# Attention scores of the latent heads: three products of 96 rows become two of 128 rows and one of 32, the last for two PSUM banks from separate rows of the array

## The chip, the core and the metric

The kernel runs on one core of a Trainium2 chip. The metric is the device time of one execution in microseconds (us). TensorE (PE) multiplies; its weight loads stand in a row of their own in a profile (PEld) and run beside its products. VectorE (DVE), ScalarE (ACT) and GpSimd (POOL) do the rest, and SyncE (SP) issues most of the DMAs.

## The reference

A decoder block on 2048 tokens of width 1024: eight heads of attention with a forget gate ("fox"), eight heads of latent attention ("mla"), an output projection, and an MLP. All arithmetic is in float32. The change touches the scores of the mla heads alone:

```
mq = concat([q_nope, q_rope])      # 64 + 32 values per head and token
mk = concat([k_nope, k_rope])      # k_rope (32 values) is the same for all heads
logits = (mq . mk) * scale ; masked ; softmax ; p . v
```

## The kernel before, in words

A float32 product is made of rounded parts. Each operand is split into a high part and a low part ("hi", "lo"), and three products are added in PSUM: hi.hi, hi.lo and lo.hi. The fourth, lo.lo, is left out.

The part of the kernel that matters is the attention stage. It works in units, each of one head and 512 queries (`qb` from 0 to 3). Fox and mla units alternate, and mla runs two units behind. A unit has score steps and value steps. A score step (`step(j, c)`, lines 809 to 833) takes 128 queries and a chunk of up to 1024 keys:

- the products of `passes` (lines 210 to 213) into one bank of PSUM, if the chunk has up to 512 keys, and otherwise into two, with half of the chunk in each (line 820);
- on DVE the mask and the row's maximum (lines 825 and 828), on ACT the exponential (829), and on POOL the scaling of the probabilities (850).

The value steps turn the probabilities with transposes on PE (870), split them into hi and lo on ACT and DVE (lines 92 and 93), and multiply them by the values (887 and 888). At the end of a unit, ACT copies the result (892), a DMA on SP's queue moves its lower half to other partitions (893), POOL adds the halves (898), and SP stores them (899).

An mla head has four operand tiles: `a` (hi of q), `b` (hi of k), `c` (lo of q), `d` (lo of k), each with 64 rows of the plain part and 32 of the rotary part. So line 820 makes three products of 96 rows for each bank: a.b, a.d and c.b. A fox head has two products for each bank, of 128 and of 66 rows, because its tiles already pack hi and lo above each other.

Tiles come from two sets of slots. `s8` has 16 slots ("big", 8 KB for each partition) and gives the heads' tiles in turn, five for each head. `s4` has 21 slots ("mid", 4 KB) and gives the probabilities; three are held for other things, so that the other 18 go round. A tile can be loaded as soon as the last reader of the slot's earlier tile is done. `mid` and `big` (`ring`) take the next slot of the round.

The order of the score and value steps comes from a sorted list of due times (`add`), but a scheduler that lays out the program moves single instructions within it, DMAs above all. On each engine the order is fixed once the program is built. SP's queue is in order: a DMA that waits holds up those behind it.

Of the kernel before, what the change touches and what calls it, by code (L numbers as in the profile page):

```python
# [9 lines left out]
F32R = mybir.dt.float32r  # L10
# [8 lines left out]
P = 128  # L19
# [21 lines left out]
def f32v(ap):  # L41
    return ap.bitcast(F32)
# [3 lines left out]
def block_kernel(ctx, tc, x, positions, attn_norm_g, w_in, b_forget, q_norm_g, w_uq, kv_norm_g, w_ukv,  # L46
# [129 lines left out]
    def load_parts(kind, h, tiles, parts):  # L176

        a, b, c, d, v = tiles
        ld = nc.sync.dma_start
        s = slice(512 * parts[0], 512 * (parts[-1] + 1))  # L180
        tt = slice(4 * parts[0], 4 * (parts[-1] + 1))
        if kind == "fox":

            if a is not None:
                ld(f32v(a[0:HD, s]), fq[0][h, :, s])
                ld(f32v(a[HD:P, s]), fq[1][h, :, s])
                ld(f32v(b[0:HD, s]), fk[0][h, :, s])
                ld(f32v(b[HD:P, s]), fk[0][h, :, s])
                ld(f32v(c[0:HD, s]), fq[0][h, :, s])
                ld(f32v(d[0:HD, s]), fk[1][h, :, s])  # L190
        else:
            g, j = divmod(h, 4)
            for q, k, i2 in ((a, b, 0), (c, d, 1)):
                ld(f32v(q[0:HD, s]), mq[i2][h, :, s])
                ld(f32v(q[HD:QKD, s]), mr[i2][g, j * ROPE:(j + 1) * ROPE, s])
                ld(f32v(k[0:HD, s]), mk[i2][h, :, s])
                ld(f32v(k[HD:QKD, s]).rearrange("r (t k) -> r t k", k=P),
                   krd[i2].rearrange("g (t r) k -> r (g t) k", r=ROPE)[:, tt])
        if v is not None:
            load_v(kind, h, v, tt)  # L200

    def load_v(kind, h, v, tt):
        nc.sync.dma_start(f32v(v[:, tt]), (fv if kind == "fox" else mv).rearrange("(t p) h d -> h p t d", p=P)[h, :, tt])
# [6 lines left out]
    def passes(kind, a, b, c, d):  # L210
        if kind == "fox":
            return [(a, b, P), (c, d, HD + 2)]
        return [(a, b, QKD), (a, d, QKD), (c, b, QKD)]

# [31 lines left out]
    def mid(shape, dt=F32):  # L248
        return s4.ring(shape, dt)
# [509 lines left out]
    with ExitStack() as es:  # L759
# [2 lines left out]
        place = [room[0][:, i] for i in range(4)] + [t[:, i] for t in room[1:3] for i in range(2)]  # L762
        halves = [room[3][0:HD, i] for i in range(2)]
        turns, due, outs = [0], [], [0]
        pss = es.enter_context(tc.tile_pool(name="pss", bufs=2, space=PSUM))
        pspt = es.enter_context(tc.tile_pool(name="pspt", bufs=4, space=PSUM))

        def load_head(kind, h):
            if (kind, h) == ("fox", 0):
                tiles = first  # L770
                s8.put(*first)
            else:
                tiles = [big([P, S]) for _ in range(4)]
            v = big([P, NT, 2 * HD])
            if h:
                load_parts(kind, h, [*tiles, v], range(4))
                if kind == "fox":
                    load_decay(h, *tiles[2:])
            elif kind == "mla":
                for i in range(4):  # L780
                    load_parts(kind, h, [*tiles, v], [i])
            else:
                for i in range(4):
                    load_v(kind, h, v, slice(4 * i, 4 * i + 4))
            return passes(kind, *tiles), v

        def cuts(t):

# [6 lines left out]

        def score_steps(head, qb, st):

            ops, _ = head
            nch = qb // 2 + 1
            st["p"] = [[] for _ in range(QB)]  # L800
            negm = sma.tile([P, QB, nch], F32, name=f"negm{nch}")
            lsum = sma.tile([P, QB, nch], F32, name=f"lsum{nch}")
            fac = sma.tile([P, QB, nch], F32, name=f"fac{nch}")
            steps = []

            def step(j, c):
                t = QB * qb + j
                k0, k1 = cuts(t)[c]
                w = k1 - k0
                prob = mid([P, 1024])  # L810
                st["p"][j].append((k0, prob))
                nb = 1 if w <= 512 else 2
                wb = w // nb
                ps = pss.tile([P, 2, 512], F32, name="ps_s")
                qs = slice(t * P, (t + 1) * P)
                wm = max(wb, 256)
                for i in range(nb):
                    kb = k0 + i * wb
                    for n, (l, r, rows) in enumerate(ops):
                        nc.tensor.matmul(ps[:, i, 0:wm], l[0:rows, qs], r[0:rows, kb:kb + wm], start=(n == 0),  # L820
                                         stop=(n == len(ops) - 1))
                src = ps[:, 0:nb, 0:wb]
                if c == nch - 1:

                    nc.vector.tensor_tensor_reduce(src, src, maskb[:, 1024 - w:].rearrange("p (b w) -> p b w", b=nb),  # L825
                                                   -1.0, -NEG, ALU.add, ALU.min, negm[:, j, c:c + 1])
                else:
                    nc.vector.tensor_reduce(negm[:, j, c:c + 1], src, AX.XY, ALU.max, negate=True)
                nc.scalar.activation(prob[:, 0:w].rearrange("p (b w) -> p b w", b=nb), src, AF.Exp,  # L829
                                     scale=-1.0 if c == nch - 1 else 1.0,  # L830
                                     bias=negm[:, j, c:c + 1], accum_out=lsum[:, j, c:c + 1])
                if c == nch - 1:
                    norm(j)

            def norm(j):
                rl = sma.tile([P, 1], F32, name="rl")
                if nch == 1:
                    nc.vector.reciprocal(rl, lsum[:, j])
                else:
                    m = sma.tile([P, 1], F32, name="mmin")  # L840
                    nc.vector.tensor_reduce(m, negm[:, j], AX.X, ALU.min)
                    nc.scalar.activation(fac[:, j], negm[:, j], AF.Exp, scale=-1.0, bias=m)
                    l2 = sma.tile([P, nch], F32, name=f"l2{nch}")
                    l1 = sma.tile([P, 1], F32, name="l1")
                    nc.vector.tensor_tensor(l2, lsum[:, j], fac[:, j], ALU.mult)
                    nc.vector.tensor_reduce(l1, l2, AX.X, ALU.add)
                    nc.vector.reciprocal(rl, l1)  # L847
                for c, (k0, k1) in enumerate(cuts(QB * qb + j)):
                    pr = st["p"][j][c][1][:, 0:k1 - k0]
                    nc.gpsimd.tensor_scalar(pr, pr, rl, 1.0 if nch == 1 else fac[:, j, c:c + 1], ALU.mult, ALU.mult)  # L850

            for j in range(QB):
                for c in range(nch):
                    steps.append(lambda j=j, c=c: step(j, c))
            return steps

        def value_steps(head, row0, qb, st):
            _, v = head
            nk = QB * qb + QB
            steps = []  # L860

# [104 lines left out]
                f()  # L966
        for t, sl in zip(room, (s8, s4, s4, s4)):
            sl.put(t)


    pz = ctx.enter_context(tc.tile_pool(name="pz", bufs=1))
# [631 lines left out]
```

## Time and profile before

| what | value |
|---|---|
| time, median of 3 runs | 2951.94 us (2951.61 to 2952.47) |
| time of the profiled execution | 2952.62 us |
| its span, first to last instruction | 2950.8 us |
| first and last product of line 820 | 558.1 and 1424.3 us from the span's start |
| PE, DVE, ACT and POOL busy over the span | 95%, 77%, 47%, 46% |
| attention stage, 700 to 1300 us: PE, DVE, ACT, POOL busy | 595.92, 539.85, 492.57, 316.33 of 600 us |

The span and the time differ by 1.8 us, which lie outside the first and the last instruction. A busy PE is counted with modelled ends of its products, which overlap one another; how much of it is really used is read from the starts of neighbouring products.

### The profile page before, as it was taken

Reading aid. Unit: us, or ns where it says so; the run is one execution under the profiler, and the core shown is the slowest. Engines: PE = TensorE matmul, PEld = TensorE weight load, DVE = VectorE, ACT = ScalarE, POOL = GpSimd, SP = SyncE. Lnnn points to the kernel's source line nnn. Section 1 sums busy time; section 2 is a strip of 40 time slices with the busy share of each in tenths; the row PEclk is TensorE's granted clock in tenths of the full one; section 3 lists DMA queues with packets and bytes.
Section 4 is the critical chain, followed back from the end, with each engine's and each line's share of the span. In section 5 each row is a group of like instructions: output and inputs, shape, how many; then the busy total and the mean of one; then the engine's idle time right before and its main releaser. Section 6 shows DMA issues by size and latency. Waiting matters only on the chain. (4 is left out here: it accounts for less than half of the span.)

```text
span 2950.8 us, 40368 instructions
## 1 busy us (share of the span) xinstructions
PE 2804.3 (95%) x14378; PEld 2378.4 (81%) x14378; DVE 2267.7 (77%) x3573; ACT 1396.8 (47%) x2485; POOL 1355.0 (46%) x896
## 2 busy tenths in 40 slices
PE   7799979989999999998899899999999999999998
PEld 7678968878888888887788678888888788878886
DVE  7867786579889889988666756667666677897898
ACT  4144223478888888886533322233223433344432
POOL 3623353345555555557532246546555333453421
PEclk9999989999999999999999999999999999999998
DMA  5364435844435335332246454465444744465551
GB/s 141 129 217 163 152 108 187 242 104 111 91 92 121 78 92 120 92 94 60 76 154 214 171 186 157 150 235 214 157 151 165 283 148 150 149 217 178 206 193 57
DMA packets 262521, 442.94 MB, mean 150 GB/s; under 512 B 41712, under 2 KB 150384, under 8 KB 255600
## 3 DMA queue, kind: packets, MB, share of 16 engines
q1 hardware_dynamic: 206848, 300.75, 34.8%
q10 hardware_dynamic: 55472, 139.61, 12.4%
q8 instruction: 114, 1.87, 0.3%
q14 instruction: 87, 0.71, 0.1%
HBM read 275.54 MB, written 156.37 MB: 146 GB/s over the span
## 5 line engine op out<-in xcount | busy, mean ns | idle before, releaser
L1260 PE MATMUL mm<-big,mid 128*128 128x512 f32 x2688 | 619.5, 392 | 17.2 <-ACT big L1335 6.9
L1260 PEld LDWEIGHTS mm<-big,mid 128*128 128x128 f32 x2688 | 506.0, 189 | 129.6 <-ACT big L1335 12.0
L127 PE MATMUL mm<-big,mid 128*128 128x512 f32 x1312 | 515.8, 394 | 8.1 <-DVE mid L236 6.5
L126 PE MATMUL mm<-big,big 128*128 128x512 f32 (+2 forms) x1160 | 437.6, 377 | 0.9 <-DVE big L236 0.9
L820 PE MATMUL ps_s<-big,big 96*128 96x384 f32 (+11 forms) x1720 | 415.4, 368 | 8.0 <-ACT mid L829 7.8
L125 PE MATMUL mm<-big,big 128*128 128x512 f32 (+2 forms) x1072 | 405.7, 378 | 12.3 <-DVE krf L388 9.8
L850 POOL TENSOR_SCALAR mid<-mid,rl,fac 128x768 f32<-128x768 f32 (+4 forms) x256 | 255.9, 1009 | 268.1 <-DVE rl L847 83.3
L829 ACT ACTIVATE mid<-ps_s,negm 128x896 f32<-128x896 f32 (+7 forms) x384 | 333.0, 868 | 93.0 <-DVE negm L825 43.6
L242 POOL TENSOR_TENSOR mid<-mid,mid 128x1024 f32<-128x1024 f32 x88 | 238.5, 2710 | 296.2 <-DVE mid L576 94.9
L235 ACT ACTIVATE big<-mid 128x1024 fp32r<-128x1024 f32 x218 | 214.9, 1049 | 319.5 <-PE mm L126 200.2
L870 PE MATMUL ps_t<-ident,mid 128*128 128x128 f32 x2176 | 339.3, 274 | 8.3 <-POOL mid L850 7.4
L870 PEld LDWEIGHTS ps_t<-ident,mid 128*128 128x128 f32 x2176 | 273.4, 141 | 63.7 <-POOL mid L850 8.2
L820 PEld LDWEIGHTS ps_s<-big,big 96*128 96x128 f32 (+2 forms) x1720 | 287.3, 192 | 30.9 <-ACT mid L829 11.8
L1171 POOL TENSOR_TENSOR mid<-mid,mid 128x1024 f32<-128x1024 f32 x60 | 199.3, 3347 | 230.8 <-DVE big L236 198.6
L127 PEld LDWEIGHTS mm<-big,mid 128*128 128x128 f32 x1312 | 249.2, 190 | 61.9 <-DVE mid L236 7.4
L236 DVE TENSOR_TENSOR mid<-mid,mid 128x1024 fp32r<-128x1024 f32 x112 | 204.5, 1850 | 116.0 <-ACT mid L235 80.1
L93 DVE TENSOR_TENSOR big<-ps_t,big 128x512 fp32r<-128x512 f32 (+3 forms) x427 | 253.7, 602 | 37.9 <-ACT big L92 34.8
L92 ACT ACTIVATE big<-ps_t 128x512 fp32r<-128x512 f32 (+3 forms) x427 | 224.8, 535 | 72.2 <-PE ps_t L870 64.9
L126 PEld LDWEIGHTS mm<-big,big 128*128 128x128 f32 x1160 | 221.8, 191 | 37.6 <-DVE big L236 1.8
L825 DVE CUSTOM_DVE_ANT_0 ps_s<-ps_s,maskb 128x768 f32<-128x768 f32 (+7 forms) x256 | 227.9, 891 | 21.5 <-PE ps_s L820 19.5
L125 PEld LDWEIGHTS mm<-big,big 128*128 128x128 f32 x1072 | 205.0, 191 | 46.3 <-DVE krf L388 10.8
L125 PE MATMUL mm<-big,mid 128*128 128x512 f32 x528 | 211.5, 401 | 6.9 <-ACT mid L991 2.4
(213 smaller groups left out, 5272.9 us busy)
## 6 DMA issues: line engine op xcount, KB each, us to landing
gd<-mid ACTq DMA_DIRECT2D x109, 512.0 KB, 3.0
mid<-gd SPq DMA_DIRECT2D x109, 512.0 KB, 3.8
mid<-in_w_up SPq DMA_DIRECT2D x64, 512.0 KB, 5.5
mid<-in_w_down SPq DMA_DIRECT2D x64, 512.0 KB, 5.1
mid<-in_x SPq DMA_DIRECT2D x32, 512.0 KB, 4.1
xd<-mid ACTq DMA_DIRECT2D x28, 512.0 KB, 2.8
big<-xd SPq DMA_DIRECT2D x14, 1024.0 KB, 8.8
mid<-in_w_in SPq DMA_DIRECT2D x24, 512.0 KB, 4.7
```

Of the source, the lines that this page charges most:

```text
L92: nc.scalar.activation(hi, ps, AF.Copy)
L93: nc.vector.tensor_tensor(lo, ps, f32v(hi), ALU.subtract)
L125: nc.tensor.matmul(ps, lh, rh, start=(k == 0), stop=False)
L126: nc.tensor.matmul(ps, lh, rl, start=False, stop=False)
L127: nc.tensor.matmul(ps, ll, rh, start=False, stop=(k == nk - 1))
L242: (eng or nc.gpsimd).tensor_tensor(t, raws[a], raws[b], op)
L820: nc.tensor.matmul(ps[:, i, 0:wm], l[0:rows, qs], r[0:rows, kb:kb + wm], start=(n == 0), stop=(n == len(ops) - 1))
L825: nc.vector.tensor_tensor_reduce(src, src, maskb[:, 1024 - w:].rearrange("p (b w) -> p b w", b=nb), -1.0, -NEG, ALU.add, ALU.min, negm[:, ...
L829: nc.scalar.activation(prob[:, 0:w].rearrange("p (b w) -> p b w", b=nb), src, AF.Exp, scale=-1.0 if c == nch - 1 else 1.0, bias=negm[:, j, ...
L850: nc.gpsimd.tensor_scalar(pr, pr, rl, 1.0 if nch == 1 else fac[:, j, c:c + 1], ALU.mult, ALU.mult)
L870: nc.tensor.transpose(ps[:, j * P:(j + 1) * P], prob[:, kt * P - k0:(kt + 1) * P - k0], ident)
L1260: nc.tensor.matmul(ps[:, m], l[:, k, tk(m)], r[:, :, tk(k)], start=(first and k == n == 0), stop=(k == 3 and n == 2), skip_group_check=True)
```

## The change

`passes` gives two products of 128 rows for an mla head. Tile `a` now holds q_nope hi above q_nope lo, and `b` holds k_nope hi twice, so that a.b is hi.hi + lo.hi of the plain part. Tile `c` holds q_nope hi, q_rope hi and q_rope lo (64 + 32 + 32 rows), and `d` holds k_nope lo and k_rope hi twice, so that c.d is hi.lo of the plain part, and hi.hi + lo.hi of the rotary part. What is left is hi.lo of the rotary part, a product of 32 rows. Its operands are `r_hi`, a new "mid" tile for each mla unit (q_rope hi, loaded twice, to rows 0 to 31 and 32 to 63), and `kr_lo`, a new "big" tile that is held during the whole stage (k_rope lo, also twice). For a chunk with two banks, the first bank uses rows 0 to 31 and the second rows 32 to 63, and the two instructions stand next to each other behind the products of 128 rows of both banks.

```diff
-            for q, k, i2 in ((a, b, 0), (c, d, 1)):
-                ld(f32v(q[0:HD, s]), mq[i2][h, :, s])
-                ld(f32v(q[HD:QKD, s]), mr[i2][g, j * ROPE:(j + 1) * ROPE, s])
-                ld(f32v(k[0:HD, s]), mk[i2][h, :, s])
-                ld(f32v(k[HD:QKD, s]).rearrange("r (t k) -> r t k", k=P),
-                   krd[i2].rearrange("g (t r) k -> r (g t) k", r=ROPE)[:, tt])
+            rows = [slice(HD + n * ROPE, HD + (n + 1) * ROPE) for n in range(2)]
+            for n in range(2):
+                ld(f32v(a[n * HD:(n + 1) * HD, s]), mq[n][h, :, s])
+                ld(f32v(b[n * HD:(n + 1) * HD, s]), mk[0][h, :, s])
+                ld(f32v(c[rows[n], s]), mr[n][g, j * ROPE:(j + 1) * ROPE, s])
+                load_rope(d[rows[n]], 0, parts)
+            ld(f32v(c[0:HD, s]), mq[0][h, :, s])
+            ld(f32v(d[0:HD, s]), mk[1][h, :, s])
...
+    def load_rope(dst, n, parts):
+        s, tt = slice(512 * parts[0], 512 * (parts[-1] + 1)), slice(4 * parts[0], 4 * (parts[-1] + 1))
+        nc.sync.dma_start(f32v(dst[:, s]).rearrange("r (t k) -> r t k", k=P),
+                          krd[n].rearrange("g (t r) k -> r (g t) k", r=ROPE)[:, tt])
...
-        return [(a, b, QKD), (a, d, QKD), (c, b, QKD)]
+        return [(a, b, P), (c, d, P)]
...
+        kr_lo = s8.get([P, S])
...
+                    for n in range(2):
+                        load_rope(kr_lo[n * ROPE:(n + 1) * ROPE], 1, [i])
...
+            r_hi = None
+            if mla is not None:
+                r_hi = mid([P, 512], F32R)
+                g, h4 = divmod(mla, 4)
+                for n in range(2):
+                    nc.sync.dma_start(f32v(r_hi[n * ROPE:(n + 1) * ROPE]),
+                                      mr[0][g, h4 * ROPE:(h4 + 1) * ROPE, 512 * qb:512 * (qb + 1)])
...
-                                         stop=(n == len(ops) - 1))
+                                         stop=(r_hi is None and n == len(ops) - 1))
+                for i in range(nb if r_hi is not None else 0):
+                    kb, rows = k0 + i * wb, slice(i * ROPE, (i + 1) * ROPE)
+                    nc.tensor.matmul(ps[:, i, 0:wm], r_hi[rows, tk(j)], kr_lo[rows, kb:kb + wm], start=False, stop=True)
```

The line numbers of the changed kernel are higher by 20 to 24: its score products stand in line 840, the new ones in 845, the transposes in 894, the value products in 911 and 912, the move of a unit's half in 917, its store in 923, and the loads of `r_hi` in 818.

How the instructions stand at three places follows. The first is on PE, where a step of an mla unit (head 2, second unit) is made; before:

```order
L820 MATMUL ps_s_8824<-big_4_8260,big_5_8259 128x320
L820 MATMUL ps_s_8824<-big_3_8262,big_5_8259 128x320
L820 MATMUL ps_s_8824<-big_4_8260,big_0_8261 128x320
L820 MATMUL ps_s_8824<-big_4_8260,big_5_8259 128x320
L820 MATMUL ps_s_8824<-big_3_8262,big_5_8259 128x320
L820 MATMUL ps_s_8824<-big_4_8260,big_0_8261 128x320
```

That is one step with two banks of 320 keys: three products for each. The same kind of step now, with what stands ahead of it (`big_7` is `kr_lo`, `mid_20_8637` is `r_hi`):

```order
L911 MATMUL ps_t_8498<-mid_0_5199,big_4_7373 128x384
L894 MATMUL ps_t_8663<-ident_63,mid_2_8265 128x128
L840 MATMUL ps_s_8644<-big_3_8303,big_0_8302 128x320
L840 MATMUL ps_s_8644<-big_8_8305,big_15_8304 128x320
L840 MATMUL ps_s_8644<-big_3_8303,big_0_8302 128x320
L840 MATMUL ps_s_8644<-big_8_8305,big_15_8304 128x320
L845 MATMUL ps_s_8644<-big_7_5202,mid_20_8637 128x320 x2
L912 MATMUL ps_t_8498<-mid_0_5199,big_4_7373 128x384
```

There are as many instructions as before, but the last two take their operands from 32 rows each, and they are neighbours. The second place is on PE directly ahead of those rows. `r_hi` takes slot 20 of the round, whose earlier tile, `mid_20_8159`, is a probability tile; the first row is its last reader:

```order
L894 MATMUL ps_t_8629<-ident_63,mid_20_8159 128x128
L894 MATMUL ps_t_8629<-ident_63,mid_9_8211 128x128
L894 MATMUL ps_t_8629<-ident_63,mid_2_8265 128x128
L840 MATMUL ps_s_8602<-big_1_7370,big_13_7369 128x512
L840 MATMUL ps_s_8602<-big_5_7372,big_2_7371 128x512
L840 MATMUL ps_s_8602<-big_1_7370,big_13_7369 128x512
L840 MATMUL ps_s_8602<-big_5_7372,big_2_7371 128x512
L912 MATMUL ps_t_8498<-big_12_5198,big_4_7373 128x512
L894 MATMUL ps_t_8656<-ident_63,mid_9_8211 128x128
L894 MATMUL ps_t_8656<-ident_63,mid_2_8265 128x128
L911 MATMUL ps_t_8498<-big_12_5198,big_4_7373 128x512
L912 MATMUL ps_t_8498<-big_12_5198,big_4_7373 128x512
```

So 17 instructions lie between the one that frees the slot and the pair that reads what is loaded into it. It is so for the second unit of heads 1 to 6; the other units have 27 or more between them. The third place is SP's queue at the start of the stage, where the first mla head's tiles (`big_1`, `big_2`, `big_5`, `big_6`, `big_13`) and then the second fox head's are loaded; before, the first unit's half (L893) stands behind the fox loads:

```order
L203 DMA big_2_5516<-mv_85 128x4x128
L185 DMA big_5_5941<-fq0_71 64x2048
L186 DMA big_5_5941<-fq1_72 64x2048
L187 DMA big_4_5942<-fk0_73 64x2048
L188 DMA big_4_5942<-fk0_73 64x2048
L189 DMA big_0_5943<-fq0_71 64x2048
L190 DMA big_3_5944<-fk1_74 64x2048
L207 DMA big_3_5944<-fb_76 2x16x128
L203 DMA big_7_5208<-fv_75 128x4x128
L893 DMA mid_13_5201<-mid_16_5200 64x512
```

Now it (L917) stands ahead of the last mla loads, and so ahead of the fox loads; the second unit's half stands behind them:

```order
L917 DMA mid_13_5201<-mid_16_5200 64x512
L197 DMA big_13_5514<-mk0_83 64x512
L198 DMA big_1_5515<-mr1_82 32x512
L208 DMA big_2_5516<-krd0_77 32x4x128
L212 DMA big_14_5209<-fv_75 128x4x128
L200 DMA big_1_5515<-mq0_79 64x512
L201 DMA big_2_5516<-mk1_84 64x512
L212 DMA big_5_5517<-mv_85 128x4x128
L185 DMA big_4_5964<-fq0_71 64x2048
L186 DMA big_4_5964<-fq1_72 64x2048
L187 DMA big_0_5965<-fk0_73 64x2048
```

The move of the first unit's half has passed the fox loads and some of the mla loads. Over the whole program SP issues 817 DMAs instead of 723.

## Rows read from the trace of the kernel before

**Rows 1.** The page: busy time, share of the span and instructions of each engine.
```profile
PE 2804.3 (95%) x14378; PEld 2378.4 (81%) x14378; DVE 2267.7 (77%) x3573; ACT 1396.8 (47%) x2485; POOL 1355.0 (46%) x896
```

**Rows 2.** Stretches of the attention stage, from:to, length, busy us of each engine.
```profile
core 0: us, PE busy (x) PEld busy (x) DVE busy (x) ACT busy (x) POOL busy (x), PEclk, DMA share, GB/s
555.00:600.00 45.00, 34.27 (x217) 29.84 (x215) 30.27 (x82) 24.59 (x62) 11.95 (x14) 0.90 0.93 251
700.00:1300.00 600.00, 595.92 (x3670) 521.68 (x3670) 539.85 (x1365) 492.57 (x1134) 316.33 (x327) 1.00 0.43 100
1300.00:1400.00 100.00, 89.03 (x519) 76.93 (x518) 87.91 (x188) 70.66 (x160) 70.49 (x62) 0.95 0.22 63
```

**Rows 3.** What PE waited for, 700 to 1300 us: total us, times, longest.
```profile
PE ps_s L820 <- ACT mid L829: 1.9, 5, 0.4
PE ps_t L888 <- DVE big L93: 1.0, 4, 0.3
PE ps_t L888 <- DVE mid L93: 0.5, 2, 0.2
```

**Rows 4.** Groups of 560 to 1425 us, shapes apart: the mla score products by width.
```profile
L820 PE MATMUL ps_s<-big,big 96*128 96x512 f32 x240 | 67.4, 411 | 0.3 <-ACT mid L829 0.3
L820 PE MATMUL ps_s<-big,big 96*128 96x448 f32 x240 | 58.3, 377 | 0.0
L820 PE MATMUL ps_s<-big,big 96*128 96x384 f32 x264 | 57.2, 349 | 0.1
L820 PE MATMUL ps_s<-big,big 96*128 96x320 f32 x240 | 45.7, 326 | 0.0
L820 PE MATMUL ps_s<-big,big 96*128 96x256 f32 x48 | 10.0, 318 | 0.5 <-ACT mid L829 0.5
```

**Rows 5.** PE in order of time: start, length, line; neighbouring starts give the pace.
```profile
902.12 0.39 PE L888 MATMUL ps_t<-mid,big 128*128 128x512 f32 x1
902.34 0.39 PE L887 MATMUL ps_t<-big,big 128*128 128x512 f32 x1
902.57 0.27 PE L870 MATMUL ps_t<-ident,mid 128*128 128x128 f32 x1
...
907.06 0.34 PE L888 MATMUL ps_t<-big,big 128*128 128x384 f32 x1
907.24 0.28 PE L887 MATMUL ps_t<-big,big 128*128 128x256 f32 x1
907.35 0.60 PE L870 MATMUL ps_t<-ident,mid 128*128 128x128 f32 x4
...
909.07 1.04 PE L870 MATMUL ps_t<-ident,mid 128*128 128x128 f32 x8
909.86 0.48 PE L888 MATMUL ps_t<-big,big 128*128 128x512 f32 x1
```

**Rows 6.** PE in order of time around a fox step, 128 and 66 rows in turn.
```profile
936.12 1.18 PE L820 MATMUL ps_s<-big,big 128*128 128x512 f32 x4
937.14 0.40 PE L888 MATMUL ps_t<-mid,big 128*128 128x512 f32 x1
```

**Rows 7.** Weight loads in order of time.
```profile
907.68 0.19 PEld L888 LDWEIGHTS ps_t<-big,big 128*128 128x128 f32 x1
907.79 0.19 PEld L887 LDWEIGHTS ps_t<-mid,big 128*128 128x128 f32 x1
907.91 0.19 PEld L888 LDWEIGHTS ps_t<-mid,big 128*128 128x128 f32 x1
```

**Rows 8.** Line 893, the small DMA of SP's queue: ns, and us from issue to landing.
```profile
L893 SPq DMA_DIRECT2D mid<-mid x64: 461/491/1472, 585.5 to 1475.8; - x64
DMA to landing us min/median/max: 2.2/2.3/12.6
```

**Rows 9.** The start of the stage: SP's DMA, POOL's wait for it, PE's wait behind.
```profile
585.53 0.53 SPq L893 DMA_DIRECT2D mid<-mid  x1
599.17 1.25 POOL L898 TENSOR_TENSOR mid<-mid,mid 64x512 f32<-64x512 f32 x1 [7.38 <-DMA mid<-mid]
601.34 0.47 PE L870 MATMUL ps_t<-ident,mid 128*128 128x128 f32 x1 [6.37 <-POOL mid L850]
```

More of the change, by code (lines that the diff above doesn't have):

```diff
@@ L784, in load_head @@
                     load_v(kind, h, v, slice(4 * i, 4 * i + 4))
-            return passes(kind, *tiles), v
+            return passes(kind, *tiles), v, None if kind == "fox" else h
         def cuts(t):
@@ L796, in score_steps @@
         def score_steps(head, qb, st):
-            ops, _ = head
+            ops, _, mla = head
             nch = qb // 2 + 1
+            r_hi = None
[5 more added lines that the diff above has]
+                                      mr[0][g, h4 * ROPE:(h4 + 1) * ROPE, 512 * qb:512 * (qb + 1)])
             st["p"] = [[] for _ in range(QB)]
@@ L857, in value_steps @@
         def value_steps(head, row0, qb, st):
-            _, v = head
+            _, v, _ = head
             nk = QB * qb + QB
@@ L968, in block_kernel @@
             sl.put(t)
+        s8.put(kr_lo)
     pz = ctx.enter_context(tc.tile_pool(name="pz", bufs=1))
```

## The prediction, made before the changed kernel ran

> **What bounds the kernel now.** Read the page first: PE is busy for 95% of the span, and the next engine, DVE, for 77% [rows 1]. That share is a mean over stages, so the second view is the table of stretches: between 700 and 1300 us, the even part of the attention stage, PE is busy for 595.92 of 600 us, DVE for 539.85, ACT for 492.57 [rows 2]. Third, the waits of that stretch: PE waited for 3.4 us in all [rows 3]. A busy PE is counted with modelled ends, so the fourth view is the order of time, where neighbouring starts give the pace: a product of 512 columns starts 0.22 to 0.23 us before the next, one of 384 columns 0.18 and one of 256 columns 0.11 [rows 5]. These are the columns at one pace and next to nothing besides. So PE is the bound here, and what leaves its queue shortens the stage. At both ends of the stage it is not so: PE is busy for 34.27 of 45 us at the start and 89.03 of 100 us near the end [rows 2].
>
> **What goes.** The number of score products stays. Of an mla step with two banks, six products of 128 or 96 rows become four and a pair of 32 rows; if the two of a pair run side by side, PE's queue is shorter by one product. The mla products are counted by width: 240 of 512 columns, 240 of 448, 264 of 384, 240 of 320, 48 of 256 [rows 4]; a third of each is the number of banks. Steps with one bank (five for each head, of widths 256, 256, 384, 512 and 512) keep three products. That leaves, for all heads, pairs of banks: 40 of 320 columns, 40 of 384, 40 of 448 and 32 of 512, which is 152 products saved. Prices by pace: 0.23 us for 512 and 0.18 for 384 [rows 5]; between those and the 0.11 of 256 I take 0.205 for 448 and 0.145 for 320. The sum is 32 x 0.23 + 40 x (0.205 + 0.18 + 0.145) = 28.6 us.
>
> Whether a pair does run side by side is shown by no row, since nothing in this trace uses 32 rows. From below a second product costs 0 (both start together), from above its whole 0.145 to 0.23 us. I take the lower end: the two share neither rows nor a bank, and weight loads already run beside products. The Trainium skill (TensorE: Matmul & The Clock Gate, Part 3) says that products in different strips of 32 rows run at once and start about 4 ns apart; by that the pairs would cost 152 x 0.004 = 0.6 us, an estimate from that page.
>
> **What is added on PE.** First, weight loads. They follow each other every 0.11 us [rows 7]. A pair needs two, 0.22 us, and only the product ahead covers them: 0.145 us at 320 columns, 0.18 at 384, 0.205 at 448, 0.23 at 512. If no load runs further ahead, 40 x (0.075 + 0.04 + 0.015) = 5.2 us stand open; if it does, 0. I take 3, near the middle, since a load can be fetched early but not always.
>
> Second, the change between 128 and 32 rows. There are 24 steps for each head, 192 in all, with two changes each, so 384. From below a change costs nothing: fox products of 128 and 66 rows alternate, and four of 512 columns take 1.02 us to the next start [rows 6], 0.255 each, of which the first carries what transposes leave open (a product behind eight transposes starts 0.79 us after the first of them [rows 5], less than eight times 0.11). From above it costs what neighbouring products now overlap, 0.39 us of length less 0.23 of pace, 0.16 us [rows 5]: 61 us in all. The nearest row is that of the fox step, also a change of rows, so I take 0; the upper end is a rival below.
>
> **What is added beside PE.** Each mla unit loads `r_hi` by two DMAs of SP's queue, 64 in all, behind which the loads of heads and the moves of unit results are queued. Their issue is about 0.49 us and landing 2.3 us after it [rows 8], so the second half is there some 2.8 us after the slot is free. For the second unit of heads 1 to 6 the slot is freed only 17 instructions ahead of the pair: two transposes, four products of 512, three more, two transposes, one product of 384, one transpose and four of 320, at the prices above 5 x 0.11 + 7 x 0.23 + 0.18 + 4 x 0.145 = 2.9 us. It is a tie: 0 to 0.5 us for each of six units, 0 to 3 us; I take 1. A unit that waits holds up PE's transposes and value products too, since PE's queue is in order. Other units have 27 or more instructions, 4 us and up, so 0.
>
> The heads' loads grow from 384 to 512 rows, and `kr_lo` takes one of the slots, so a fox head's last operand tile is loaded later than before, but still well over a hundred PE instructions ahead; DMA engines are busy for 0.43 in the even part [rows 2]. I take 0.
>
> At the start DMA is full (0.93 [rows 2]), and more is loaded there: 18 more issues on SP (eight of the first mla head, eight of `kr_lo`, two of `r_hi`), at about 0.5 us each, 9 us, delay the loads of the second fox head, which is read only after the first mla unit. But the move of the first unit's half no longer stands behind the fox loads. Before it was issued at 585.53, POOL's addition began only at 599.17, after 7.38 us of waiting, and PE stood for 6.37 us behind that [rows 9]. The second unit's half now stands behind the same loads instead, so the wait may move on as well as go. From -6 to +6 us; I take 0.
>
> **What eats into the gain.** DVE has 60 us free of 600 [rows 2]; with PE's part shorter by some 3%, its share rises from 90% to 93%, and short waits of PE get more frequent. For them I take a tenth of the gain, 3 us (0 to 10). Near the end (1300 to 1400 us) PE already has 11 us free, so half of the last head's share, 28.6 / 8 / 2 = 1.8 us, is lost.
>
> **The sum.** -28.6 + 3 + 0 + 1 + 0 + 3 + 1.8 = -19.8 us. The profiled execution took 2952.6 us, of which the span was 2950.8 and 1.8 lie outside it; that stands 0.7 us over the median of the runs, 2951.9. So 2932.8 by the profiled execution, 2932.1 by the median; I say 2933.
>
> **The rivals.** The first ends on the other side: each change between 128 and 32 rows empties the array, so that the next product cannot start until the last has left. For it speaks the length of a product over its pace, 0.16 us [rows 5], which must be hidden somehow; against it the free alternation of 128 and 66 rows [rows 6], which may however be one and the same setting. The place is the two ends of every pair. It decides from 19.8 / 384 = 0.05 us for each change; at 0.16 us the time is 2933 + 61 = 2994. If the weight loads too wait for the empty array, 0.11 us more for each change [rows 7], 42 us, it is 3036. The Trainium skill (TensorEngine Tiling (Array Packing), Tiling Modes) says that changing the tiling mode, as against the tile, drains TensorE; it gives no time for it. No row of this trace can show it agree or not.
>
> Second, the change doesn't do what it says: the two of a pair run one after the other. Then 28.6 us are not won, and only the small costs are left: 2952.6 + 1 = 2954, or up to 2957 with open weight loads. For it: no row with two products at once. Against it: separate rows and banks.
>
> Third, the changes cost a part, 0.03 to 0.06 us, and the gain is mostly gone: 2944 to 2956.
>
> Fourth, the gain is there on PE, but DVE and ACT, whose steps each chunk needs in turn, take over as the bound: of 28.6 us a third is left, and 2943 comes out. For it: DVE at 90% and ACT at 82% in the even part [rows 2]; against it: PE waited for 3.4 us of 600 [rows 3].
>
> **How the numbers follow.** My forecast has 0.40, with 2922 to 2945 as its own range: the lower end with no open weight loads, no lost tenth and the wait at the start gone, the upper end with the small costs at their bounds. Draining at 0.06 us or more has 0.32, the pair in series 0.09, the partial cost 0.12 and DVE as the bound 0.07. Faster by over 0.2% (under 2946; about 0.2% is what a measurement of this kernel can tell from no change): the forecast, the fourth and a part of the third, 0.51. Within 0.2%: the rest of the third and most of the second, 0.15. Slower: 0.34. The range goes from 2922 to 2998, so that the drain at its price of 0.16 us lies in it, and the drain with open weight loads does not (0.12); 0.04 lie below.
>
> **What would show it.** In order of time, the two of a pair start within some 0.02 us, and the next product follows one pace after: step right. A start of the second a whole pace after the first: the second rival. A gap ahead of the pair and behind it that no wait explains: the first; PE's count of busy us in the stage would then not fall. Waits of PE's line 845 for a DMA, in the second units of heads: the tie went wrong. DVE or ACT as what PE waits for, well over 3.4 us in 600: the fourth. A stage between first and last score product (866 us now) that is not some 20 us shorter makes the prediction wrong.

## The result: 3.1% slower

The changed kernel takes 3044.23 us (median of 4 runs, 3042.51 to 3047.0), the kernel before 2951.78 (4 runs, 2950.85 to 2952.47). The ratio is 1.0314 with an interval of 1.0296 to 1.0332: 92 us more, where 19 less were forecast. The time lies outside the range.

Nearly all of it lies in the attention stage: line 840's first and last product stand at 559.6 and 1513.7 us, 954 us apart, where they were 866 apart. What comes behind is 1 us longer than before.

The page after, to be set beside [rows 1]:

```profile
PE 2864.3 (94%) x14378; PEld 2359.4 (78%) x14378; DVE 2264.8 (74%) x3573; ACT 1401.0 (46%) x2485; POOL 1355.3 (45%) x896
```

PE has as many instructions as before and 60 us more of busy time, although 304 of its products run in pairs. The stretches of the stage, with the columns of [rows 2]:

```profile
555.00:600.00 45.00, 37.06 (x230) 32.09 (x228) 31.70 (x81) 24.07 (x60) 14.65 (x17) 0.92 0.91 261
700.00:1300.00 600.00, 566.24 (x3248) 450.03 (x3246) 477.39 (x1206) 439.06 (x1004) 279.95 (x287) 0.97 0.45 102
1300.00:1400.00 100.00, 92.95 (x533) 73.94 (x533) 78.07 (x196) 71.57 (x164) 44.41 (x49) 0.97 0.39 88
```

In the even part PE starts 3248 products in 600 us instead of 3670, stands for 34 us instead of 4, and is granted 0.97 of its clock instead of 1.00. The start of the stage is a little better than before. Two things have to be told apart here: PE that is busy and gets less done, and PE that waits.

**Busy and slower.** The order of time around a pair, PE and its weight loads (PEld) after, in the place of [rows 5, 6]:

```profile
972.99 0.83 PE L840 MATMUL ps_s<-big,big 128*128 128x320 f32 x4
...
973.75 0.18 PEld L845 LDWEIGHTS ps_s<-big,mid 32*128 32x128 f32 x2 [0.19 <-issue]
973.75 0.41 PE L845 MATMUL ps_s<-big,mid 32*128 32x320 f32 x2
974.10 0.19 PEld L912 LDWEIGHTS ps_t<-big,big 128*128 128x128 f32 x1 [0.16 <-DVE rl L871]
974.10 0.44 PE L912 MATMUL ps_t<-big,big 128*128 128x384 f32 x1
...
974.38 0.49 PE L894 MATMUL ps_t<-ident,mid 128*128 128x128 f32 x3
```

The two of the pair share one start (the single records are 0.003 us apart). But from their start to the next product 0.35 us go by, for 320 columns that take 0.145 at the pace of the prediction. The value product behind them, of 384 columns, takes 0.28 to the next start instead of 0.18. And the weight loads of both start when the product itself does (973.75, 974.10), not during the product ahead. No wait on another engine's work explains it: the release named is "issue", or an instruction of DVE that had ended at 973.86, 0.24 us before.

**Waiting.** What PE waited for from 700 to 1300 us, in the place of [rows 3]:

```profile
PE ps_s L845 <- DMA mid<-mr: 27.6, 10, 5.0
PE ps_t L912 <- DVE big L93: 2.3, 6, 0.5
PE ps_t L912 <- DVE mid L93: 1.6, 4, 0.6
```

The new wait is the one for `r_hi`; the others are hardly changed. From 555 to 1530 us it comes to 34.4 us in 13 waits. Six of them are near 5 us, one for each of heads 1 to 6; the other seven, 0.6 to 1.3 us, belong to first units but for one. One of the six, in order of time on SP's queue and on PE:

```profile
741.85 0.31 SPq L818 DMA_DIRECT2D mid<-mr  x1
...
745.51 0.31 SPq L818 DMA_DIRECT2D mid<-mr  x1
...
749.16 0.70 PE L840 MATMUL ps_s<-big,big 128*128 128x512 f32 x2
...
754.38 0.79 PE L845 MATMUL ps_s<-big,mid 32*128 32x512 f32 x1 [4.51 <-DMA mid<-mr]
...
755.10 0.80 PE L912 MATMUL ps_t<-big,big 128*128 128x512 f32 x1
```

This is the third unit of its head, not the second. The first half of `r_hi` was issued at 741.85, behind the next mla head's loads, and PE goes on 12.5 us later. The last of those loads was issued at 737.41 and landed at 753.86, `r_hi` behind it at 754.34. From 732 to 755 us the packets of queue q1 take 90.1% of the time of the 16 DMA engines:

```profile
q1 hardware_dynamic: 2912, 4.72, 90.1%
```

The line's own record, beside [rows 8], says the same of the worst landing:

```profile
L818 SPq DMA_DIRECT2D mid<-mr x64: 307/323/852, 460.2 to 1480.6; - x64
...
DMA to landing us min/median/max: 1.8/3.4/12.5
```

What follows the wait is as dear again by half. A product of 512 columns now lasts 0.80 us instead of 0.39 [rows 5]. The stretches behind two of the six waits:

```profile
755.00:760.00 5.00, 5.00 (x18) 3.82 (x17) 2.04 (x4) 1.87 (x4) 2.45 (x3) 0.50 0.34 78
875.00:880.00 5.00, 5.00 (x18) 3.82 (x17) 2.04 (x4) 1.86 (x4) 2.56 (x3) 0.50 0.34 78
```

The granted clock is 0.50 there, the level of 1.2 GHz, after PE had stood for 4.5 to 5 us; the six such stretches have 0.50 to 0.59. Five us at half clock are 2.5 us of work, six times some 15 us, an estimate from these rows.

At the start of the stage the move of the first unit's half is issued at 582.62 instead of 585.53. POOL's addition, which waits for it, begins at 595.64 instead of 599.17 and without the 7.38 us of waiting, and no product behind it waits for POOL, where one stood for 6.37 us [rows 9]:

```profile
582.62 0.50 SPq L917 DMA_DIRECT2D mid<-mid  x1
...
595.64 1.26 POOL L922 TENSOR_TENSOR mid<-mid,mid 64x512 f32<-64x512 f32 x1
```

### The profile page after: what moved, and what is told of

Read it like the earlier page. It is cut to its first block, busy times and chain, and to the rows that moved or that the text cites. A ratio compares the mean times of both kernels' runs of the same rounds, so it can differ in the third digit from the quotient of the medians.

```text
span 3041.6 us, 40519 instructions
## 1 busy us (share of the span) xinstructions
PE 2864.3 (94%) x14378; PEld 2359.4 (78%) x14378; DVE 2264.8 (74%) x3573; ACT 1401.0 (46%) x2485; POOL 1355.3 (45%) x896
## 5 line engine op out<-in xcount | busy, mean ns | idle before, releaser
L840 PE MATMUL ps_s<-big,big 128*128 128x384 f32 (+4 forms) x1376 | 355.5, 376 | 3.2 <-ACT mid L853 3.0
L894 PE MATMUL ps_t<-ident,mid 128*128 128x128 f32 x2176 | 348.6, 278 | 3.0 <-POOL mid L874 2.7
L840 PEld LDWEIGHTS ps_s<-big,big 128*128 128x128 f32 x1376 | 228.3, 194 | 19.3 <-ACT mid L853 5.7
```

The source lines that it names most:

```text
L894: nc.tensor.transpose(ps[:, j * P:(j + 1) * P], prob[:, kt * P - k0:(kt + 1) * P - k0], ident)
```

## The experiments

Each kernel ran beside the kernel before on the same chip. "us more" or "less" of a kernel by itself is its ratio to before, times 2952; between two kernels, the difference of their ratios. Such a difference has an interval of 7 to 11 us either way.

Beside the time, the order of the steps matters. The traces give it as a list, between the first and the last score product, of transposes, value products by width and score steps by width. "In common" is the share of two such lists that stands in the same order in both.

### Without the late r_hi: the pair, full rows, the same rows, nothing (e1 to e4)

e1 loads `r_hi` two units ahead into tiles of its own, two mid slots that leave the round:

```diff
+        early = [s4.get([P, 2, 512]) for _ in range(2)]
+
+        def r_hi_of(k):
+            return early[k // 2 % 2][:, k % 2]
...
-                r_hi = mid([P, 512], F32R)
...
+                k = 4 * mla + qb
+                r_hi = r_hi_of(k)
+                for ahead in ((0, 1, 2) if k == 0 else (2,)):
+                    fetch_r_hi(k + ahead)
```

> The changed kernel, but r_hi has four tiles of its own and is loaded two units ahead. Theory: two costs ate the gain, the change between 128 and 32 rows (0.09 us for the array to empty and 0.11 for an uncovered weight load, 384 times, 76 us) and the late r_hi (PE waited 34.4 us for it, and ran at a granted clock of 0.50 behind the six long waits, some 3 us each). Without the second, 3044 - 34 - 18 = 2992 us (2985 to 3000), and no wait of PE for this DMA. Rival (the waits only take the place of others, all is in the row changes): 3030 us or more. Rival (late data is most of it): under 2965 us.

Measured: 2973.18 us, ratio 1.0066 (1.0044 to 1.0087). PE's waits for `r_hi` are gone. All three guesses missed: it is 73 us under the changed kernel, where the theory had 52, one rival 14 or less and the other over 79. But two slots leave the round here, which changes the order too (e5 to e12). e2 is e1 with a third product of 128 rows for each bank (`kr_lo` zero below its 32 rows), so that nothing changes rows and nothing runs in pairs:

```diff
-                    kb, rows = k0 + i * wb, slice(i * ROPE, (i + 1) * ROPE)
+                    kb, rows = k0 + i * wb, slice(0, P)
```

> As the run before, with r_hi early, but the third product has 128 rows for either bank, of which rows 32 to 127 are zero: the same products, tiles and order, no change between row counts, no pair. Theory (the row change costs 0.2 us each time): as the kernel before, 2950 to 2960 us, and next to no gaps around the third product. Rival (the gaps come with the product's place, its operands or its bank, not with its rows): 2952 + 76 = 3028 us or so.

Measured: 2920.69 us, ratio 0.9888 (0.9862 to 0.9915). So the pair with its changes of rows costs 52 us more than the full rows that it was to improve on, with nearly the same order on PE (99% in common). But e2 is also 33 us faster than before, which neither theory had, and which e5 takes up. e3 is e1 with both small products in rows 0 to 31, so that they can't run side by side:

```diff
-                    kb, rows = k0 + i * wb, slice(i * ROPE, (i + 1) * ROPE)
+                    kb, rows = k0 + i * wb, slice(0, ROPE)
```

> r_hi early, and both products of 32 rows use rows 0 to 31, so that they cannot run side by side; the number of changes between 128 and 32 rows is the same. Theory (the pair does run side by side and saves 28 us): 28 us over the run with r_hi early, or more if the second weight load is uncovered too (152 x 0.1 = 15 us). Rival (the pair saves nothing): the same time as the run with r_hi early.

Measured: 3002.23 us, ratio 1.0159 (1.0128 to 1.0191), 27 us over e1 by the ratios, with the very same order: as expected, the pair does save its 28 us. The price of the change of rows can be read between e2 and e3, whose order on PE is nearly the same (99% in common). PE in order of time, a step with two banks of 448 columns, and the weight load of the product behind it; e2:

```profile
970.76 1.06 PE L853 MATMUL ps_s<-big,big 128*128 128x448 f32 x4
971.66 0.57 PE L858 MATMUL ps_s<-big,mid 128*128 128x448 f32 x2
971.87 0.19 PEld L924 LDWEIGHTS ps_t<-big,big 128*128 128x128 f32 x1
972.07 0.39 PE L924 MATMUL ps_t<-big,big 128*128 128x512 f32 x1
```

and e3:

```profile
965.61 1.06 PE L850 MATMUL ps_s<-big,big 128*128 128x448 f32 x4
966.60 0.68 PE L855 MATMUL ps_s<-big,mid 32*128 32x448 f32 x2
967.20 0.19 PEld L922 LDWEIGHTS ps_t<-big,big 128*128 128x128 f32 x1 [0.32 <-issue]
967.21 0.38 PE L922 MATMUL ps_t<-big,big 128*128 128x256 f32 x1
```

The small products start 0.99 us behind the four large ones instead of 0.90, and the product after them 0.61 us later instead of 0.41. So 0.09 us go on entering the section of 32 rows, and 0.20 inside it and on leaving: 0.11 [rows 7] for the weight load that starts only with the product, which leaves 0.09. The 0.10 that the next product loses was seen above: its weight load, which in e2 begins 0.20 us ahead of it, begins with it here. That is 0.39 us for a step, 0.2 for each change, and for 192 steps 75 us; less the 28 of the pairs, 47 are left, and 52 were measured. The single records of all the sections of e1 and e3 give the same at every width, a median of 0.09 us on entering, 0.19 inside and on leaving, and 0.10 at the product behind (0.06 where that has 128 columns).

e4 leaves the third product out, and with it q_rope hi by k_rope lo; it shows what leaving that product out gives:

```diff
-            if mla is not None:
+            if False:
                 r_hi = mid([P, 512], F32R)
```

> Leaves out the product of hi of the rotary query and lo of the rotary key (the third product of each bank), and with it r_hi; two products of 128 rows for each bank are left. Theory (PE's queue bounds the stage, a product saved is time saved): 344 products of mean 0.185 us, 63 us less than before, 2888 us (2885 to 2900). Rival (DVE takes over as the bound): half of it, 2920 us.

Measured: 2909.74 us, ratio 0.9851 (0.983 to 0.9872). Of the 63 us only 44 come out. The order on PE has 92% in common with the kernel before, so this is no clean price of the products. And PE waits again from 700 to 1300 us:

```profile
PE ps_t L912 <- DVE l L870: 13.0, 6, 2.8
PE ps_t L912 <- DVE big L93: 2.1, 4, 0.5
```

### The order of the steps (e5, e10, e11, e12)

e5 is the kernel before, with its three products of 96 rows, and three slots held out of the rounds, unused:

```diff
+        held = [s8.get([P, S]), *[s4.get([P, 2, 512]) for _ in range(2)]]
```

> The kernel before, with its three products of 96 rows, but with three slots taken out of the rounds for the whole stage (one big, two mid) and nothing put into them, as many as the kernel with 128-row third products (2920.7 us, ratio 0.989) holds. With fewer slots the same score and value steps come in another order on PE, much the order of that kernel. Theory A (that kernel's gain of 33 us over before is the order of the steps, not the packing): 2915 to 2930 us, ratio 0.988 to 0.993. Rival B (128 rows in place of 96, or the other loads, give it): the time of before, ratio 0.997 to 1.003.

Measured: 2928.54 us, ratio 0.9907 (0.9887 to 0.9927). Theory A: 27 of e2's 33 us come with no change of arithmetic at all, and the order on PE has 97% in common with e2, where the kernel before has 86%. The even part of e5, with the columns of [rows 2]:

```profile
700.00:1300.00 600.00, 599.83 (x3753) 533.39 (x3752) 540.58 (x1391) 502.25 (x1159) 319.96 (x330) 1.00 0.43 100
```

PE starts 3753 products in 600 us instead of 3670, 2.3% more. The 4 us in which PE stood idle are gone; the other 9 or 10 us come of products that start sooner behind one another, which I did not split further. e10 holds only the two mid slots, e11 four mid slots, and e12 is e2 with two more:

```diff
+        held8, held4 = [s8.get([P, S]) for _ in range(0)], [s4.get([P, 2, 512]) for _ in range(2)]
```

> The kernel before with two mid slots held out and unused, and no big one. Theory A (the gain of 28 us with three slots held, ratio 0.991, comes of the mid slots, a round of 16 probability tiles instead of 18): 2920 to 2935 us, ratio 0.988 to 0.994. Rival B (it comes of the big slot, the heads' tiles): the time of before, ratio 0.997 to 1.003.

> The kernel before with four mid slots held out and unused, a round of 14. Theory A (a shorter round lets the scores run less far ahead and takes waits from PE, further still with 14): below 2925 us, ratio under 0.99. Rival B (16 happens to give a good order; with 14 the scores wait for slots): at or above 2935 us, ratio 0.994 or more, with more waits of PE.

> The version with the third product over 128 rows (zeros in 96 of them) and r_hi in tiles of its own, two further mid slots held out and unused, a round of 14 instead of 16 (with 16: 2920.7 us, ratio 0.989). Theory A (a shorter round is better): under 2915 us, ratio under 0.987. Rival B (a round of 14 makes the scores wait): above 2925 us, ratio over 0.99.

Measured: e10 2936.5 us, ratio 0.9938 (0.9915 to 0.996); e11 2960.5 us, 1.0018 (1.0007 to 1.0028); e12 2953.73 us, 1.0003 (0.9989 to 1.0016). Most of the gain comes of the mid slots (e10: 18 of 27 us), but a round of 16 gives a good order and 14 does not: in both tries rival B. It is no rule that shorter rounds are better.

### What counts as a change of rows (e6, e7)

e6 is e2 with the third product over 64 rows, half of them zeros:

```diff
-                    kb, rows = k0 + i * wb, slice(0, P)
+                    kb, rows = k0 + i * wb, slice(0, 2 * ROPE)
```

> The third product over 64 rows instead of 128 (half of them zeros), one for each bank, loaded early. Order on PE as with 128 rows (2920.7 us, ratio 0.989). Theory A (64 rows is a section of the array like 32, so that each step pays two changes of about 0.2 us, 192 steps): 76 us more, 2997 us, ratio 1.015, as with both products in the same 32 rows (1.016). Rival B (64 rows go like the 66 of a fox head, only 32 is a change): 2921 us, ratio 0.989.

Measured: 2990.85 us, ratio 1.012 (1.0102 to 1.0138), 69 us over e2 by the ratios: 64 rows pay like 32. The two kernels have the very same order on PE and, but for the rows of the third product, the same instructions there, so that only these rows are left to explain the 69 us; that is 0.36 us for each of 192 sections, beside the 0.39 read above. PE in order of time, as for e2 and e3:

```profile
961.65 1.05 PE L853 MATMUL ps_s<-big,big 128*128 128x448 f32 x4
962.62 0.68 PE L858 MATMUL ps_s<-big,mid 64*128 64x448 f32 x2
963.23 0.39 PE L925 MATMUL ps_t<-big,big 128*128 128x256 f32 x1
```

The same 0.61 us as in e3. The fox products of 66 rows beside 128 cost nothing like it [rows 6]. The Trainium skill (TensorEngine Tiling (Array Packing), Tiling Modes) lists 128, 64 and 32 rows as the three settings of the array; the trace agrees that 64 is not the setting of 128, and shows that 66 rows go with 128.

e7 is e1 with each small product directly behind its own bank, so that a step with two banks enters and leaves twice:

```diff
-                for i in range(nb if r_hi is not None else 0):
-                    kb, rows = k0 + i * wb, slice(i * ROPE, (i + 1) * ROPE)
-                    nc.tensor.matmul(ps[:, i, 0:wm], r_hi[rows, tk(j)], kr_lo[rows, kb:kb + wm], start=False, stop=True)
+                    if r_hi is not None:
+                        rows = slice(i * ROPE, (i + 1) * ROPE)
+                        nc.tensor.matmul(ps[:, i, 0:wm], r_hi[rows, tk(j)], kr_lo[rows, kb:kb + wm], start=False, stop=True)
```

> As the early-loaded pair (2973 us, ratio 1.0066), the same order on PE, but each 32-row product directly behind the 128-row products of its own bank, so that the 152 steps with two banks enter and leave the 32-row section twice and the products no longer run side by side. Theory A (the price is 0.2 us for each change, entering and leaving): 152 x 0.4 = 61 us more, and 28 us for the products in series, 3062 us, ratio 1.037. Rival B (the price is one for each step, whatever the number of changes, such as for a first use of the operands): only the 28 us, 3001 us, ratio 1.016.

Measured: 3052.77 us, ratio 1.0333 (1.0311 to 1.0355), 79 us over e1 by the ratios, with the very same order of steps, where A said 89 and B 28. A step with two banks of 320 columns, in order of time on PE:

```profile
975.06 0.46 PE L850 MATMUL ps_s<-big,big 128*128 128x320 f32 x2
975.45 0.41 PE L854 MATMUL ps_s<-big,mid 32*128 32x320 f32 x1
975.79 0.56 PE L850 MATMUL ps_s<-big,big 128*128 128x320 f32 x2
976.28 0.41 PE L854 MATMUL ps_s<-big,mid 32*128 32x320 f32 x1
976.62 0.33 PE L921 MATMUL ps_t<-big,big 128*128 128x128 f32 x1
```

Each small product, alone now, takes 0.34 us to the next start, the same as a whole pair after the change (0.35). The price is for each entry and exit.

### Why r_hi was late (e8, e9, e13, e14)

e8 is e1 with each `r_hi` asked for where its unit begins:

```diff
-                for ahead in ((0, 1, 2) if k == 0 else (2,)):
-                    fetch_r_hi(k + ahead)
+                fetch_r_hi(k)
```

> As the early-loaded pair (2973 us, ratio 1.0066), with the same tiles of its own for r_hi, free for two units, but each loaded when its unit begins instead of two units ahead. Theory A (r_hi is late because of what stands ahead of its DMA in SP's queue and among the head loads, not because its slot comes free late): 25 to 70 us more, 2998 to 3043 us, ratio 1.015 to 1.03. Rival B (it was late because the slot's last reader stood 17 instructions ahead; or what looked like lateness was the order of the steps with a round of more slots): 2973 to 2980 us, ratio 1.007 to 1.009.

Measured: 2976.38 us, ratio 1.0071 (1.0048 to 1.0094), as B said. But it was no test of A, since the loads weren't late at all. Its DMAs of `r_hi`:

```profile
L785 SPq DMA_DIRECT2D mid<-mr x64: 302/312/690, 552.2 to 1345.8; - x64
...
DMA to landing us min/median/max: 1.8/5.7/13.9
```

They land no sooner after their issue than in the changed kernel. But the last is issued at 1345.8 instead of 1480.6: nothing holds them back, and the scheduler has put them far ahead (each by 34 us or more, from issue to the unit's first pair). e9 is the changed kernel with two mid slots held out, `r_hi` still taking its slot from the round:

```diff
         kr_lo = s8.get([P, S])
+        held = [s4.get([P, 2, 512]) for _ in range(2)]
```

> The changed kernel word for word (r_hi takes a mid slot of the round for each unit), with two mid slots held out of the round and unused, so that the round has 16 as in the kernels that load r_hi into tiles of its own (2973 and 2976 us, ratio 1.007). Theory A (r_hi is late because its slot comes free only behind the last reader of a probability tile, close ahead of the pair): PE still waits for the DMA of r_hi, 20 us or more in total, and the time is 3005 to 3035 us, ratio 1.017 to 1.027. Rival B (all of the 71 us between the changed kernel and those was the order of the steps with a round of 18): 2970 to 2985 us, ratio 1.005 to 1.01, with few such waits.

Measured: 3057.24 us, ratio 1.0343 (1.0324 to 1.0361), 80 us over e8 by the ratios, above even A's range. PE from 700 to 1300 us waits much as in the changed kernel:

```profile
PE ps_s L846 <- DMA mid<-mr: 22.5, 10, 5.1
PE ps_s L841 <- ACT mid L854: 8.6, 20, 0.7
```

So with `r_hi` in a slot of the round the waits are there, with 16 slots as with 18. The 80 us are no clean price of them, since the order has only 89% in common with e8. The last two take the slot and the queue apart without the order of 16. e13 is e1 with `r_hi` in one big slot, and the probabilities keep 18.

```diff
-        early = [s4.get([P, 2, 512]) for _ in range(2)]
+        early = s8.get([P, 4, 512])
...
-            return early[k // 2 % 2][:, k % 2]
+            return early[:, k % 4]
```

> As the early-loaded pair, but r_hi takes one big slot in place of two mid ones, so that the round of probability tiles keeps its 18 and the order of the steps is much that of the kernel before (and not the better one with 16). Theory A (entering and leaving the 32-row section costs 76 us, the pair gives 28 back, and the order gives nothing here): 2995 to 3005 us, ratio 1.014 to 1.018; then the late r_hi is the rest to the changed kernel, 40 to 50 us. Rival B (the round of 16 gave the early-loaded kernels nothing, unlike the kernel before): 2970 to 2980 us, ratio 1.006 to 1.009, and the late r_hi costs 65 to 75 us.

Measured: 2983.66 us, ratio 1.0101 (1.0086 to 1.0116), between the two. Its order has 99% in common with the kernel before, so in that order the scores' own change costs 30 us. The changed kernel's order has only 87% in common with either, so the other 63 us (1.0314 less 1.0101) are the late `r_hi` and another order together. e14 leaves the slot and issues the two DMAs from POOL's queue:

```diff
-                    nc.sync.dma_start(f32v(r_hi[n * ROPE:(n + 1) * ROPE]),
+                    nc.gpsimd.dma_start(f32v(r_hi[n * ROPE:(n + 1) * ROPE]),
```

> The changed kernel with the two DMAs of r_hi issued from POOL's queue instead of SP's; its slot is still one of the round. Theory A (what stands ahead in SP's queue, the store of the unit before above all, makes the second half of r_hi late): PE's waits for r_hi fall from 34 us to under 15 us, and the time to 3010 to 3025 us, ratio 1.02 to 1.025. Rival B (the slot comes free too late, whichever queue the DMA is in): 30 us or more of waits, 3035 to 3060 us, ratio 1.028 or more.

Measured: 3040.53 us, ratio 1.0289 (1.0272 to 1.0307). Neither: PE waits only 0.5 us for `r_hi`, as A said, and the time is all but that of the changed kernel, as B said. The wait has moved. All engines in order of time at the place of the 5 us wait, beside the next mla head's loads:

```profile
761.40 1.26 POOL L922 TENSOR_TENSOR mid<-mid,mid 64x512 f32<-64x512 f32 x1 [8.58 <-DMA mid<-mid]
...
763.79 0.17 DVE L862 RECIPROCAL rl<-lsum 128x1 f32<-128x1 f32 x1 [5.10 <-POOL mid L874]
...
764.58 0.69 ACT L853 ACTIVATE mid<-ps_s,negm 128x512 f32<-128x512 f32 x1 [4.67 <-DVE negm L852]
...
765.41 0.90 PE L840 MATMUL ps_s<-big,big 128*128 128x320 f32 x2 [3.26 <-ACT mid L853]
```

POOL stands for 8.58 us before its addition, for the small move of a unit's half. Its scaling is late, then DVE, then ACT, then PE. The order on PE is another one here (89% in common with the changed kernel), and the move of that half is now what is late among the head's loads: from 555 to 1530 us POOL waits 60.7 us for such moves, and 37.1 in the changed kernel; PE waits 26.5 us for ACT's exponentials, and 3.0 there.

So the slot alone does not make PE wait for `r_hi`: with the same slot and another queue that wait is gone. SP's queue alone does not either: with slots of its own and SP's queue it is gone as well (e1, e8), because the load is then issued long before the head's loads. In these runs it took both, a slot that keeps the load from being issued early and the bulk loads ahead of it in the queue. The time is not won back by the other queue.

## Why the prediction was wrong

Right were that the two of a pair run side by side (one start; 27 us lost in e3 without it, and 28.6 was the sum) and that the start of the stage moves by less than 6 us: PE is busy there for 37.06 of 45 us instead of 34.27 [rows 2]. That DVE and ACT don't take over as the bound was not put to the test, since PE got slower; in e4, where PE has less to do, it waits 13.0 of 600 us for one line of DVE.

**The step that failed first** is "the change between 128 and 32 rows", of which I said "so I take 0". It costs 0.2 us, 384 times: 0.09 us on entering, as much on leaving, and a weight load of 0.11 us each way that no product covers. That is rival one with open weight loads, put there at 0.27 us for each change and 3036, with its size a third too high. That 3036 lies near the measured time is luck: it holds nothing of the late `r_hi`, and too much for the changes. The nearest row was of 128 and 66 rows in turn, and I wrote myself that these "may however be one and the same setting"; e6, where 64 rows pay what 66 don't, bears that out. With it falls "I take 3" for the weight loads: I counted what a short product leaves open of two loads, and left to the rival that they could not run ahead at all. The scores' change then costs 30 us by e13, 52 by e1 against e2, and by the prices 75 - 28 = 47, where the forecast had -26.

**The second** is "the second half is there some 2.8 us after the slot is free ... Other units have 27 or more instructions, 4 us and up, so 0". I took the median landing of 2.3 us, and the 12.6 stood in the same row [rows 8]. The second units of heads 1 to 6, for which I had the tie, don't wait; the third units do, whose `r_hi` is issued behind the next head's loads, 12.5 us before PE goes on and with as long a landing, and the first units a little. Beside the waits stands what I did not price at all, half the clock for some 5 us after each long one. Of the 63 us, 34 are waits and some 15 the clock; the other 14 are not assigned, and the changed order may be in them.

**What was missing** from the sum is the order. That I counted a moved instruction only by what it waits for left out that a change in the slots shifts all score and value steps: with the same arithmetic it gave -27 us (e5, three slots held out) or +5 (e11, four). The changed kernel's round still has 18, of which each mla unit now takes one for `r_hi`, and its order has only 87% in common with the kernel before. What that is worth by itself no run shows; why the scores' change measures 30 us in one order and 52 in another stays open too.

What would have shown the rival was named: "a gap ahead of the pair and behind it that no wait explains". PE's busy time in the even part did fall, though, from 595.92 to 566.24 us, because of the waits; it was the number of products started that told.

The fastest version found that computes the whole is e2, 2920.69 us, 1.1% under the kernel before: two products of 128 rows and a third over 128 rows with zeros, which saves no product and has its gain mostly from the order.

## What to carry to other kernels

A short section of 32 or 64 rows among products of 128 costs 0.4 us to enter and leave, about two products of 448 columns. It pays only where one section holds enough products side by side to save more than that; here it saved one, and padding with zeros was better. A small load that is needed soon should neither wait for a slot of a shared round nor stand behind bulk loads; in e14 another queue for it only moved the wait to another small transfer. Price it by its longest landing, and add the slow clock that a PE idle for 5 us is left with.

## What was not expected of the hardware

Weight loads, which elsewhere run beside the product ahead, start with the product itself both in the section of 32 rows and directly behind it (973.75 and 974.10 above; in e2, with 128 rows, 971.87 for a product at 972.07). A section of 64 rows costs the same as one of 32 (0.61 us for two products of 448 columns and the way out, against 0.41 with 128 rows), while 66 rows among 128 keep the pace: before, the next product starts a median of 0.149 us behind one of 66 rows and 320 columns, and 0.147 behind one of 96 rows in a row of such.
